# The conv branch of a hybrid encoder layer by Strassen's scheme, two gate groups at a time

## The chip, the cores and the metric

One core of one Trainium2 chip. The metric is the device time of one launch in microseconds, the median of several runs; smaller is better. The engines are TensorE (PE; its weight loads are shown as PEld), VectorE (DVE), ScalarE (ACT), GpSimd (POOL) and SyncE (SP), which here issues all DMAs of the stages that matter.

## The reference

One layer on x (1024 tokens x 1024), all in float32:

```python
u = rms_norm(x, norm1_g)
q, k, v, cb, cc, ch, ga, gb = split(u @ w_in)      # 3 x 512, 3 x 512, 2 x 1024
y_a = neighbourhood_attention(rms(q), rms(k), v, rpb) @ w_attn_branch     # 512 -> 1024
y_b = (cb * conv3(cc * ch)) @ w_conv_branch                              # 512 -> 1024
x = x + (sigmoid(ga) * y_a + sigmoid(gb) * y_b) @ w_o
x = x + square(relu(rms_norm(x, norm2_g) @ w_mlp_in)) @ w_mlp_out
```

The change concerns `y_b = b @ w_conv_branch` with `b = cb * conv3(cc * ch)`, and how its weights and those of the gates `ga`, `gb` are prepared beside the products.

## The kernel before

Every float32 product is made from f16 pairs: an operand is scaled by a power of two and split into a high and a low part (ScalarE copies the high part, VectorE subtracts it for the low one), and three passes of matmuls, high x high, low x high and high x low, are added up in PSUM. A unit is the group of matmuls that fills one PSUM bank; `unit` emits its matmuls (L236) and then moves the two background lists on by some steps: `fg`, work that is soon needed, and `bg`, the preparation of later weights, `ticks` steps a unit. So the order of all instructions is fixed when the program is built, and each engine works through its own list strictly in that order.

The preparation of a weight chunk, called a chain below: SyncE loads 512 KB into one of five `raw` tiles (L259) as soon as the tile's last reader is done; ScalarE scales it by rows (L1099) and sums its squares (L1108), or VectorE takes its largest absolute value (L362); a 128x1 matmul with a column of ones (L227, "ones matmul") sums over the partitions; VectorE makes a power of two of it; ScalarE and VectorE write the f16 high and low parts (L343 and L330, or L1238 and L1234). The ones matmul stands in TensorE's list between two units.

The stages: norm and transposes; V, Q, K projections; attention with the conv projections between its steps; gates and branches; O; two halves of the MLP. In the stage of the gates and branches the 1024 output channels are taken in eight groups of 128 (gate n = 0 to 7). Gate 0 (chunk G) is a plain product in units of 24 matmuls. Gates 1 to 7 (chunks S1 to S7) go by Strassen's scheme with seven units of 12 matmuls: the token halves and K halves of u stand ready in seven forms (`FORM`), made by DMA transposes from `gs` into `uT`, `QR` and `s4T`, and each gate's weights get seven forms: GpSimd makes the sums (`gsum`, L1221), `parts` splits them. After each gate come its branch units: attention (weights w_a, chunk A of two gate groups) and conv (weights w_b, chunk B), two token halves each, 12 matmuls a unit, plain. `post` multiplies by the gate, adds to `m`, and `m_done` scales and splits `m` for the O stage.

The conv rows of step j (0 to 3: 128 conv channels by 1024 tokens) are scaled, put in token order and split into the f16 pair `BT[:, w, j]` (bT in the profile) by `conv_split` during attention.

Of the kernel before, what the change touches and what calls it, by code (L numbers as in the profile page):

```python
# [18 lines left out]
D = 1024  # L19
# [9 lines left out]
def plan():  # L29
# [8 lines left out]
    branch = lambda j: [((k, j), block(w, [(256 * j, 256)], 4, 4)) for k, w in (("A", "w_a"), ("B", "w_b"))]  # L38
    for n in range(8):
        p.append((("S" if n else "G", n), block("w_in", [(3072 + 128 * n, 128), (4096 + 128 * n, 128)], 4)))  # L40
        if n % 2 == 0:
            p += branch(n // 2)
# [57 lines left out]
def encoder_block(ctx: ExitStack, tc: tile.TileContext, x, weights, cols, gqk, rel, masks, out):  # L100
# [745 lines left out]
    def conv_post(j, g, half, ps, d):  # L846
# [19 lines left out]
        cv = d["cv"]  # L866
        V.tensor_tensor(perm(cv, half), p3, perm(cv, half), op=OP.mult)
        if half == 1:
            conv_tail.append(conv_split(j, cv))
# [15 lines left out]
    def conv_split(j, cv):  # L885
        ch = cConv[j]
        m, s, inv = tmp(), tmp(), tmp()
        A.activation(BT[:, 1, j].bitcast(BF16), cv, AF.Square, accum_out=sc[:, m])
        yield
        V.tensor_scalar(sc[:, m], sc[:, m], 1e-36, None, op0=OP.max)  # L890
        yield
        yield from pow2_half(m, 14, s, inv)
        mul(inv, ch.inv, at(rowsB, j))
        if j == 3:
            for c in cB:
                c.ready = True
        G.tensor_scalar(cv, cv, sc[:, s], 1.0, op0=OP.mult, op1=OP.mult)
        yield
        bh, bl = (BT[:, w, j].rearrange("p (b r c) -> p b r c", b=8, r=16) for w in range(2))
        A.activation(bh, perm(cv), AF.Copy)  # L900
        yield
        pv = perm(cv)
        for b in range(0, 8, 2):
            G.tensor_tensor(bl[:, b:b + 2], pv[:, b:b + 2], bh[:, b:b + 2], op=OP.subtract)

    def conv_mms(first):

        for j in range(4):
# [3 lines left out]
            if 0 < j < 3:  # L912
                push(cConv[j + 1])
            elif j == 3:
                side[0], held[0] = True, 1
                push(cG, cA[0], cB[0])
# [155 lines left out]
    def turn_piece(i, o, m):  # L1072
        n, s = m // 2, m % 2
        SP.dma_start_transpose(free(o)(s)[:, :, 128 * n:128 * n + 128], GS[:, n, i, s])
# [61 lines left out]
    def deal(k):  # L1136
        room = 216.0 * share(k) + 520.0
        if conv_tail and not advance(conv_tail[0]):
            conv_tail.pop(0)
        for n in range(4):  # L1140
            if n and any(debt[i] + m.ns - mark[i] > room - 200.0 for i, m in enumerate(meters)):
                return
            tick(1)

    for k in range(N + 13):
# [28 lines left out]
        if 35 <= k < 59 and k % 3 == 2:  # L1174
            turn_piece(1, 0, (k - 35) // 3)
        if 69 <= k < 77:
            turn_piece(2, 2, k - 69)
# [13 lines left out]
    V, A = nc.vector, nc.scalar  # L1191
    solo[0] = False
# [4 lines left out]
    wpool["wa"] = wpool["wb"] = p3.enter_context(tc.tile_pool(name="wab", bufs=2))  # L1197
# [3 lines left out]
    actB = lambda s, k: BT[:, s, k]  # L1201
# [10 lines left out]
    turn_s(3, 6)  # L1212
# [15 lines left out]
    def parts(todo, s, then):  # L1228

        prev = None  # L1230
        for n, it in enumerate(todo + [None]):
            if prev:
                o, w = prev
                V.scalar_tensor_tensor(o(1), w, sc[:, s], o(0), op0=OP.mult, op1=OP.subtract)  # L1234
                then(n - 1)
            if it:
                o, w = it
                A.activation(o(0), w, AF.Copy, scale=sc[:, s])  # L1238
# [12 lines left out]

    def prep_s(n):

        ch = cS[n]
        t = w3p.tile([128, 4, 512], F32, name="gsum", bufs=1)
        if n == 1:
            while ch.s is None:
                yield WAIT
            yield from forms_sum(ch, t, None)
            s = ch.s  # L1260
        else:
            yield from rows_scaled(ch, g1)
            yield from forms_sum(ch, t, 2)
            s, ch.inv = yield from scale_of(ch.sum, 9, 2)
        while done[0] < ch.first:
            yield WAIT
        ch.P = wsp.tile([128, 7, 2, 512], F16, name="w16_s", tag="ws")
        yield from forms_split(ch, t, s, ch.P)
        ch.split = True
# [15 lines left out]
    def m_split(n, m, s):  # L1285
        A.activation(M[0][:, n], m, AF.Copy, scale=sc[:, s])
        yield
        V.scalar_tensor_tensor(M[1][:, n], m, sc[:, s], M[0][:, n], op0=OP.mult, op1=OP.subtract)

    def m_done(n, m):  # L1290
        mx, s = tmp(), tmp()
        V.tensor_reduce(sc[:, mx], m, axis=AX, op=OP.max, apply_absolute_value=True)
        yield
        yield from pow2(mx, 14, s, at(rowsM, n))
        yield from m_split(n, m, s)

    def gate_units(n, tail=None):
# [20 lines left out]
        def post3(ps):  # L1318
# [9 lines left out]
            7: post7, 3: post3}, 2, 4 if n < 7 else 6, (1, 6, 2, 4, 5, 7, 3))  # L1328
        return sg

    def branch_units(n, post, mid=None):
        j, cc = n // 2, (n % 2) * 128
        for g, act, ch in ((0, actA, cA[j]), (1, actB, cB[j])):
            built(ch)
            for half in range(2):
                ps = anybank()
                unit(ch_mms(ps, act, half, ch, 4, 256, cc),
                     lambda ps=ps, g=g, half=half, ch=ch: post(g, half, ps, sc[:, ch.inv]), 2, 4)
                if mid and g == 0 and half == 0:
                    mid()  # L1340

    for n in range(8):
        built(cG if n == 0 else cS[n])
        if n < 7:
            bg.append(prep_s(n + 1))
        m = w3p.tile([128, 2, 512], F32, name="m", bufs=1)
        mf = m.rearrange("p a t -> p (a t)")
        if n < 7:
            sg = gate_units(n)
            if n:  # L1350
                sg = [sg[:, i] for i in range(4)]
            if n in (1, 3, 5):
                push(cA[n // 2 + 1], cB[n // 2 + 1])

            def post(g, half, ps, iv, sg=sg, m=m):
                t = sg[2 * half + g]
                V.scalar_tensor_tensor(t, ps, iv, t, op0=OP.mult, op1=OP.mult)  # L1357
                if g == 1:
                    V.tensor_tensor(m[:, half], sg[2 * half], t, op=OP.add)
            branch_units(n, post, (lambda: turn_s(0, 2)) if n == 0 else None)  # L1360
            if n == 0:
                late.append(lambda: held.__setitem__(0, 0))
            late.append(lambda n=n, mf=mf: fg.append(m_done(n, mf)))
        else:
            push(cO[0])
            tick(4)
            y = w3p.tile([128, 4, 512], F32, name="gsum", bufs=1)
            branch_units(n, lambda g, half, ps, iv: A.activation(y[:, 2 * half + g], ps, AF.Copy, scale=iv))
            settle()
            drain()  # L1370
            s7 = tmp()

            def bound():
                mm, m2, mx = tmp(4), tmp(2), tmp()
                V.tensor_reduce(sc[:, mm], y, axis=AX, op=OP.max, apply_absolute_value=True)
                yield
                V.tensor_tensor(sc[:, m2], sc[:, mm.start:mm.start + 4:2], sc[:, mm.start + 1:mm.start + 4:2],
                                op=OP.add)
# [647 lines left out]
```

## Time and profile before

| | |
|---|---|
| time, median of 3 runs | 1200.63 us (1200.57 to 1201.13) |
| profiled execution | 1201.78 us |
| its span, first to last instruction | 1200.0 us |
| granted TensorE clock | 1.00 |
| PE busy | 1190.2 us, 99%, 6272 instructions |
| DVE, ACT, POOL busy | 78%, 63%, 38% |
| gates 1 on start at (timeline) | 332.13 us |
| O stage starts at (timeline) | 532.48 us |

A row of a group gives the line of the kernel, the engine, the operation, output and inputs by their names, sizes and count, then busy time and mean duration, then the idle time before it with what ended it. A row of a timeline gives the start, the duration, the same names, and in brackets the engine's idle time before it. SPq is SyncE's own queue: the time that an issue holds it.

### The profile page before, as it was taken

What the parts mean: (1) busy time and instruction counts of PE and PEld (TensorE: products, weight loads), DVE (VectorE), ACT (ScalarE), POOL (GpSimd) and SP (SyncE); (2) the same over time, 40 slices, a digit from 0 to 9 for tenths busy, and PEclk for the clock granted to TensorE, in tenths of its full rate; (3) what the DMA queues carried; (4) which work ended last, traced back from release to release, by engine and by line L of the source; (5) the groups of instructions that cost most, each with busy time, mean ns of one, the idle gap of its engine ahead of it and who ended that gap; (6) DMA issues with size and microseconds to landing.
All of it is one profiled execution on the core that took longest, in us unless ns stands there. A gap on an engine that the chain in (4) does not pass through costs nothing.

```text
span 1200.0 us, 16982 instructions
## 1 busy us (share of the span) xinstructions
PE 1190.2 (99%) x6272; PEld 574.7 (48%) x6272; DVE 940.3 (78%) x1750; ACT 752.1 (63%) x1181; POOL 450.9 (38%) x296
## 2 busy tenths in 40 slices
PE   8999999999999999999999999999999999999998
PEld 7444444444444444444467444444444444444444
DVE  7987878899558786877888645645548999999998
ACT  7765668778654545337778778678675843746440
POOL 5610022322311203001014665565567561564562
DMA  7745547576641121234397445435466925435202
GB/s 259 201 153 126 107 96 145 124 163 117 135 121 58 54 70 36 71 116 165 60 170 195 174 142 192 160 130 193 153 242 220 356 73 193 158 120 214 105 36 105
DMA packets 162707, 171.25 MB, mean 143 GB/s; under 512 B 123328, under 2 KB 123840, under 8 KB 158528
## 3 DMA queue, kind: packets, MB, share of 16 engines
q1 hardware_dynamic: 162624, 170.17, 48.4%
q8 instruction: 49, 0.80, 0.3%
q14 instruction: 34, 0.28, 0.1%
HBM read 102.51 MB, written 37.75 MB: 117 GB/s over the span
## 4 chain that ended last, share of the span: by engine, by line
PE 84%; DVE 11%; ACT 2%; issue 1%; DMA 1%; SPq 0%; ACTq 0%
PE ps_d L236 27%; PE ps_s L236 24%; PE ps_o L236 20%; PE ps_d L1067 5%; PE ps_d L669 2%; PE ps_d L718 2%; PE ps_s L718 2%; DVE P L95 2%; PE ps_s L669 2%; DVE w_s L1234 1%; DVE sz L95 1%; DVE sc L95 1%; DVE w_ws L95 1%; DVE sg L1357 1%; DMA xt<-in_x 1%
## 5 line engine op out<-in xcount | busy, mean ns | idle before, releaser
L236 PEld LDWEIGHTS <-ops 128*128 128x128 f16 x1356 | 132.5, 98 | 157.3
L236 PEld LDWEIGHTS <-w 128*128 128x128 f16 x1368 | 132.8, 98 | 139.4
L1067 PE MATMUL ps_d<-uT,w_ws 128*128 128x512 f16 x576 | 128.0, 379 | 0.3 <-DVE cv L95 0.3
L236 PE MATMUL ps_s<-ops 128*128 128x512 f16 (+1 forms) x504 | 114.3, 376 | 0.0
L236 PE MATMUL ps_d<-ops 128*128 128x512 f16 x492 | 112.9, 379 | 0.0
L236 PE MATMUL ps_d<-u2T,w 128*128 128x512 f16 (+1 forms) x504 | 110.1, 371 | 0.0
L1847 ACT ACTIVATE ops<-hf,sc 128x2048 f16<-128x2048 f32 x26 | 52.0, 1998 | 84.8 <-PE ps_d L236 47.2
L1221 POOL TENSOR_TENSOR tsum<-raw 128x512 f32<-128x512 f32 x28 | 48.2, 1737 | 139.3 <-DVE v L1475 74.2
L1425 POOL TENSOR_TENSOR as<-as 128x512 f32<-128x512 f32 x60 | 82.9, 1382 | 41.6 <-ACT as L1707 38.1
L236 PEld LDWEIGHTS <-w_s 128*128 128x128 f16 x588 | 56.8, 98 | 69.0 <-DVE w_s L1234 1.2
L1067 PEld LDWEIGHTS <-w_ws 128*128 128x128 f16 x576 | 54.6, 98 | 65.6 <-issue 1.5
L236 PE MATMUL ps_o<-ops 128*128 128x512 f16 (+1 forms) x360 | 81.3, 375 | 0.0
L236 PE MATMUL ps_s<-u2x,w 128*128 128x512 f16 (+1 forms) x348 | 78.6, 375 | 0.0
L1849 DVE SCALAR_TENSOR_TENSOR ops<-hf,sc,ops 128x2048 f16<-128x2048 f32 x26 | 74.8, 2876 | 3.2 <-ACT ops L1847 2.2
L1099 ACT ACTIVATE raw<-raw,sc 128x256 f32<-128x256 f32 x164 | 67.5, 494 | 1.9 <-DMA raw<-in_weights 1.9
L1221 POOL TENSOR_TENSOR gsum<-raw 128x512 f32<-128x512 f32 x14 | 19.3, 1394 | 127.8 <-issue 53.6
L1238 ACT ACTIVATE w<-raw,sc 128x512 f16<-128x512 f32 (+1 forms) x28 | 24.6, 927 | 50.8 <-DVE sc L475 50.8
L1740 DVE TENSOR_TENSOR as<-ps_s,as 128x512 f32<-128x512 f32 x13 | 9.0, 692 | 57.9 <-ACT as L1759 57.9
L1321 ACT ACTIVATE sg<-sg,sc 128x2048 f32<-128x2048 f32 (+1 forms) x7 | 13.2, 1880 | 52.2 <-DVE sg L1319 52.2
L1863 POOL TENSOR_TENSOR raw<-raw 128x1024 f32<-128x1024 f32 x8 | 30.8, 3870 | 36.5 <-DVE ops L1857 36.5
L236 PE MATMUL ps_o<-u2T,w 128*128 128x512 f16 (+1 forms) x204 | 44.2, 366 | 0.0
L236 PEld LDWEIGHTS <-mH 128*128 128x128 f16 x304 | 29.6, 98 | 30.4
(393 smaller groups left out, 2664.2 us busy)
## 6 DMA issues: line engine op xcount, KB each, us to landing
raw<-in_weights SPq DMA_DIRECT2D x89, 512.0 KB, 5.2
hs<-as SPq DMA_DIRECT2D x16, 1792.0 KB, 8.7
hf<-hs SPq DMA_DIRECT2D x26, 1024.0 KB, 6.6
w2x<-in_weights SPq DMA_DIRECT2D x16, 512.0 KB, 7.6
raw<-in_weights SPq DMA_DIRECT2D x16, 384.0 KB, 3.7
xt<-in_x SPq DMA_DIRECT2D x8, 512.0 KB, 10.2
gs<-s SPq DMA_DIRECT2D x4, 1024.0 KB, 4.4
x<-in_x SPq DMA_DIRECT2D x8, 512.0 KB, 10.6
```

The lines of the kernel that those rows point to most:

```text
L95: return f(out, *a, **kw)
L236: T.matmul(ps, l, r, start=a, stop=b)
L669: T.matmul(ps, UT[:, sa, k, b * 128:(b + 1) * 128], w, start=(kind, k) == ("hh", 0), stop=(kind, k) == ("hl", 7))
L718: T.matmul(vbank["q", b], UT[:, sa, k, b * 128:(b + 1) * 128], cQ.parts[:, sw, 512 * k:512 * k + 512], start=(k, n) == (0, 0), stop=(k, n) ...
L1067: T.matmul(ps, l, r, start=a, stop=b)
L1099: A.activation(v, v, AF.Copy, scale=sc[:, at(g, 4 * i + k)])
L1221: G.tensor_tensor(t[:, o], a, b, op=OP.add)
L1238: A.activation(o(0), w, AF.Copy, scale=sc[:, s])
L1425: sub.tensor_tensor(z[o], z[a], z[b], op=op)
L1847: A.activation(P[:, 1, 0], hf, AF.Copy, scale=sc[:, Rs])
L1849: V.scalar_tensor_tensor(P[:, 1, 1], hf, sc[:, Rs], P[:, 1, 0], op0=OP.mult, op1=OP.subtract)
L1863: G.tensor_tensor(w11[i2], w11[i2], w12[i2], op=OP.add)
```

## The change

The conv branch is made by Strassen's scheme over K (two halves: steps j of even and odd number), tokens (two halves) and output channels (two gate groups). For each of the four pairs of gate groups there are seven units of 6 matmuls in place of four units of 12.

- `conv_split` and `conv_forms` make seven forms of the conv rows for each half a = j // 2: per half two scalings, four sums and seven low parts on GpSimd, seven high copies on ScalarE, staged in four slots, and seven puts of 256 KB to a DRAM tile `BF` (bf in the lists).
- `land` reads a form back (512 KB) into one of four slots of the old bT space, four units ahead; it is issued once the unit that last read the slot is emitted.
- `prep_b` makes seven forms of a pair's w_b: ScalarE's squares, a ones matmul, four sums on GpSimd, eight splits.
- `ab(j)` emits a pair's B units and the four A units in a written order; `zb` holds the conv branch's four quarters; the addition of the two gated branches moves from VectorE to GpSimd (`join`); `m_done` takes ScalarE's sum of squares in place of VectorE's largest value, and `m` stays where the gates' products are.
- All chains S1, B0, S2, A1, S3, B1 and on go into one list `bg` at the stage's start. The loads of B chunks stand behind those of the odd S chunks.
- Gate 0 takes its second token half first, and its eight `uT` transposes follow that half; the transposes to `QR` and `s4T` are made with 8 x 128 columns in place of 4 x 128 (half as many). Gate 1 has its own order of units, 1, 6, 2, 4, 7, 5, 3. A0's units stay between gate 0 and gate 1; pair 0's B units come after gate 1.

```diff
+    def conv_forms(a, r):
+        for e in range(2):
+            G.tensor_scalar(CF[:, e], CF[:, e], sc[:, at(r, e)], 1.0, op0=OP.mult, op1=OP.mult)
...
+        hi(0, o1), hi(1, e0), hi(2, o0)
+        yield
+        lo(0, o1), lo(1, e0), lo(2, o0)
+        yield
+        G.tensor_tensor(o1, e1, o1, op=OP.subtract)
+        hi(3, o1)
+        yield
+        G.tensor_tensor(e1, e0, e1, op=OP.subtract)
+        G.tensor_tensor(e0, o1, e0, op=OP.subtract)
+        yield
+        put(0, 3), put(1, 0), put(2, 1)
+        lo(3, o1)
...
-    turn_s(3, 6)
+    for n in range(4):
+        SP.dma_start_transpose(s4T.rearrange("p s k t -> p (s k) t")[:, :, 128 * n:128 * n + 128],
+                               GS[:, n, 3].rearrange("p s c -> p (s c)"))
...
+    def prep_b(j):
+        ch = cB[j]
+        while not ch.raw or not formed[1]:
+            yield WAIT
...
+        for a in range(2):
+            A.activation(M[1][:, 6, :512].bitcast(BF16), raw[:, 512 * a:512 * a + 512], AF.Square,
+                         scale=sc[:, at(rowsB, a)], accum_out=sc[:, at(sm, a)])
+        yield
+        am = sum_of(sm)
...
-            for half in range(2):
+            for half in (1, 0):
                 ps = anybank()
                 unit(ch_mms(ps, actU, half, cG, 8, 256, 128), ...
+                if half:
+                    turn_s(0, 2)
...
+    def land(g):
+        if g < 28:
+            SP.dma_start(SLOT[:, g % 4], BF[:, SEVEN[ORDB[g % 7]][0]])
...
+        def b_unit(o):
+            i = ORDB[o]
+            w = {5: 6, 6: 5}.get(SEVEN[i][1], SEVEN[i][1])
+            act = SLOT[:, (7 * j + o) % 4]
+            ps[i] = anybank()
+            unit(group(ps[i], [(P[:, w, sw, 128 * a:128 * a + 128], act[:, a, sa]) for a in range(2)
+                               for sw, sa in PASSES]), posts.get(i), 2, 4)
+            land(7 * j + o + 4)
+        order = "bb0b1bbb2b3"
+        if j == 0:
+            order = "bbb2bb3bb"
...
+    bg.append(prep_s(1))
+    bg.append(prep_b(0))
+    for j in range(1, 4):
+        bg.append(prep_s(2 * j))
+        push(cA[j])
+        if j < 3:
+            bg.append(prep_s(2 * j + 1))
+        bg.append(prep_b(j))
```

The lists of the two programs give 12546 rows on TensorE before and 12498 now: 24 matmuls and 24 weight loads fewer. Three places show what moves.

SyncE from the last attention transposes to gate 1. Before, where raw_3679 and raw_3744 are the two parts of S2, raw_3773 is A1 and raw_3775 B1:

```order
L1023 DMA_TRANSPOSE PT_3463<-P16_3460 128x8x128
L1074 DMA_TRANSPOSE qD_965<-gs_112 128x4x128 x8
L1210 DMA_TRANSPOSE s4T_3634<-gs_112 128x4x128 x8
L259 DMA raw_3679<-in_weights 128x1024
L259 DMA raw_3744<-in_weights 128x1024
L1210 DMA_TRANSPOSE uT_109<-gs_112 128x4x128 x8
L259 DMA raw_3773<-in_weights 128x1024
L259 DMA raw_3775<-in_weights 128x1024
```

Now, where raw_3667 and raw_3723 are the parts of S2, raw_3725 is A1, bf the forms' puts and bT<-bf the first reads:

```order
L1119 DMA_TRANSPOSE qD_965<-gs_112 128x8x128 x2
L1260 DMA_TRANSPOSE s4T_3622<-gs_112 128x8x128 x4
L261 DMA raw_3667<-in_weights 128x1024
L922 DMA bf_1659<-bT_1197 128x1024 x3
L1257 DMA_TRANSPOSE uT_109<-gs_112 128x4x128 x8
L922 DMA bf_1659<-bT_1197 128x1024
L261 DMA raw_3723<-in_weights 128x1024
L261 DMA raw_3725<-in_weights 128x1024
L922 DMA bf_1659<-bT_1197 128x1024 x3
L1441 DMA bT_1197<-bf_1659 128x2048 x4
```

The second load of S2 and that of A1 stand behind the eight uT transposes, and puts stand between; the first load waits for the last of w_a's low parts.

VectorE at the start of gate 1. Before, between the end of m's chain and the first sums of gate 1 (sg_3811), one cast for a ones matmul, that of S2:

```order
L1326 TENSOR_TENSOR sg_3811<-ps_s_3840,sg_3811 128x512
L1288 SCALAR_TENSOR_TENSOR mL_3633<-m_3643,sc_71,mH_3632 128x1024
L1327 TENSOR_TENSOR sg_3811<-ps_o_3861,sg_3811 128x512
L1079 TENSOR_REDUCE sc_71<-sc_71 128x1
L1080 CAST ones_72<-sc_71 128x1
L1310 TENSOR_TENSOR sg_3811<-ps_o_3906,sg_3811 128x512
```

Now, from S1's last splits (w16_s_3678) on; the first cast is B0's, the next A1's, the last S2's:

```order
L1284 SCALAR_TENSOR_TENSOR w16_s_3678<-gsum_3673,sc_71,w16_s_3678 128x2x512 x2
L364 TENSOR_REDUCE sc_71<-raw_3725 128x4
L1468 SCALAR_TENSOR_TENSOR raw_3483<-ps_s_3734,sc_71,raw_3483 128x512
L1124 TENSOR_REDUCE sc_71<-sc_71 128x1
L1125 CAST ones_72<-sc_71 128x1
L152 TENSOR_TENSOR sc_71<-sc_71 128x4
L372 TENSOR_REDUCE sc_71<-sc_71 128x1
L374 CAST ones_72<-sc_71 128x1
L1468 SCALAR_TENSOR_TENSOR raw_3483<-ps_o_3762,sc_71,raw_3483 128x512
L1124 TENSOR_REDUCE sc_71<-sc_71 128x1
L1125 CAST ones_72<-sc_71 128x1
```

Three casts stand together behind the reduction of A1's load, ahead of gate 1's first sum; on TensorE B0's ones matmul stands right behind gate 1's first unit, where before no ones matmul came until six units of gate 1 were through.

ScalarE around the end of gate 1. Before, with gate 1's sigmoid first, S2's splits (w16_s_3959), the scaling of S3 (raw_3964, raw_3966) and its squares:

```order
L1321 ACTIVATE sg_3811<-sg_3811,sc_71 128x2048
L1238 ACTIVATE w16_s_3959<-raw_3679,sc_71 128x512
L1238 ACTIVATE w16_s_3959<-raw_3744,sc_71 128x2x512
L1238 ACTIVATE w16_s_3959<-gsum_3828,sc_71 128x2x512 x2
L1099 ACTIVATE raw_3964<-raw_3964,sc_71 128x2x128 x4
L1099 ACTIVATE raw_3966<-raw_3966,sc_71 128x2x128 x4
L1108 ACTIVATE gsum_4043,sc_71<-raw_3964 128x1024
L1108 ACTIVATE gsum_4043,sc_71<-raw_3966 128x1024
```

Now, with S2's splits (w16_s_3937) ahead of the sigmoid, S3 in raw_3890 and raw_3942, A1's high parts (w16_wa_3991) and B1's squares (raw_3944):

```order
L1288 ACTIVATE w16_s_3937<-gsum_3932,sc_71 128x2x512 x2
L1426 ACTIVATE sg_3786<-sg_3786,sc_71 128x2048
L1144 ACTIVATE raw_3890<-raw_3890,sc_71 128x2x128 x4
L1144 ACTIVATE raw_3942<-raw_3942,sc_71 128x2x128 x4
L1153 ACTIVATE mL_3621,sc_71<-raw_3890 128x1024
L1512 ACTIVATE zb_3627<-ps_d_3949 128x512
L345 ACTIVATE w16_wa_3991<-raw_3725,sc_71 128x256 x4
L1153 ACTIVATE mL_3621,sc_71<-raw_3942 128x1024
L1338 ACTIVATE mL_3621,sc_71<-raw_3944,sc_71 128x512 x2
```

S3's scaling now follows the sigmoid at once, with the chains of A1 and B1 in the same stretch; the cast that B1's ones matmul waits for needs the last row.

More of the change, by code (lines that the diff above doesn't have):

```diff
@@ L37, in plan @@
     p += [(("C", j), block("w_in", [(c + 128 * j, 128) for c in (2048, 2560, 1536)])) for j in range(4)]
[L38 removed]
+    branch = lambda k, w, j: (((k, j), block(w, [(256 * j, 256)], 4, 4)))
     for n in range(8):
@@ L1342, in encoder_block @@
[L1342 to L1363, printed above, removed]
+    ORDB = (1, 6, 2, 4, 5, 7, 3)
```

328 lines of the change are left out of this document (236 added, 92 removed).

## Prediction

> **What bounds the kernel now.** I read the page first: the busy times and the chain that ended last.
>
> ```profile
> span 1200.0 us, 16982 instructions
> ...
> PE 1190.2 (99%) x6272; PEld 574.7 (48%) x6272; DVE 940.3 (78%) x1750; ACT 752.1 (63%) x1181; POOL 450.9 (38%) x296
> ...
> PE 84%; DVE 11%; ACT 2%; issue 1%; DMA 1%; SPq 0%; ACTq 0%
> ```
>
> TensorE is busy for 99% of the span, so anything that takes a matmul away pays, and anything that makes TensorE wait costs in full. Then the table by stage, for the last 60 us of attention and the first gates (busy us, count, granted clock, DMA share).
>
> ```profile
> 240.00:270.00 30.00, 30.00 (x216) 14.61 (x213) 27.64 (x74) 22.33 (x53) 7.02 (x9) 1.00 0.77 163
> 270.00:300.00 30.00, 29.69 (x220) 14.89 (x220) 29.59 (x89) 24.84 (x62) 8.66 (x10) 1.00 0.65 117
> 330.00:360.00 30.00, 30.00 (x141) 13.58 (x140) 17.08 (x32) 15.00 (x26) 5.66 (x4) 1.00 0.43 121
> ```
>
> In the gates TensorE has no gap and VectorE is at 57%: there is room on average, and what decides is the moment at which each weight chain is ready. The timeline of TensorE at the place of the change, with its longest wait near the start of the program:
>
> ```profile
> 8.37 0.62 PE L598 MATMUL ps_o<-ident,u 128*128 128x128 f16 x8 [2.30 <-POOL u L585]
> ...
> 326.95 2.75 PE L236 MATMUL ps_d<-bT,w_wb 128*128 128x512 f16 x12
> 329.54 2.75 PE L236 MATMUL ps_s<-bT,w_wb 128*128 128x512 f16 x12
> 332.13 2.75 PE L236 MATMUL ps_d<-uT,w_s 128*128 128x512 f16 x12
> ```
>
> A unit of 12 matmuls starts 2.59 us after the one before, 0.216 us a matmul. Gate 1 starts at 332.13.
>
> **What is removed.** The conv branch has 8 x 2 x 12 = 192 matmuls before and 4 x 7 x 6 = 168 after. 24 x 0.216 = 5.2 us off TensorE. Two of the old B units stood ahead of gate 1 and now stand behind it, so gate 1 begins at 326.95 and its first unit ends at 329.54, on before's clock.
>
> **Gate 1, first stall.** Behind that unit stands the ones matmul of the first B chunk. It waits for VectorE's cast, and VectorE reaches the cast only past the reduction over the first part of A1's weights (raw_3725), whose load SyncE issues behind eight uT transposes; the squares that feed the cast stand on ScalarE behind the scaling of gate 2's second part (raw_3723), whose load stands behind them too. Before, both loads of gate 2 stood ahead of those transposes:
>
> ```profile
> 314.44 11.07 SPq L1210 DMA_TRANSPOSE s4T<-gs x8
> 325.62 0.99 SPq L259 DMA_DIRECT2D raw<-in_weights x2
> 326.70 10.36 SPq L1210 DMA_TRANSPOSE uT<-gs x8
> 337.17 1.46 SPq L259 DMA_DIRECT2D raw<-in_weights x3
> ```
>
> A transpose holds SyncE for 1.3 us, a load for 0.5. The rows for the rest of the chain, from the timelines of ScalarE, GpSimd and VectorE:
>
> ```profile
> 312.59 1.71 ACT L343 ACTIVATE w_wa<-raw,sc 128x256 f16<-128x256 f32 x4 [0.31 <-POOL bT L904]
> 329.86 3.30 ACT L1099 ACTIVATE raw<-raw,sc 128x256 f32<-128x256 f32 x8 [1.88 <-DMA raw<-in_weights]
> 307.72 1.12 POOL L897 TENSOR_SCALAR cv<-cv,sc 128x1024 f32<-128x1024 f32 x1 [10.71 <-DVE sc L95]
> 309.57 0.35 DVE L95 TENSOR_TENSOR sc<-sc 128x1 f32<-128x1 f32 x2
> 313.13 5.30 DVE L330 SCALAR_TENSOR_TENSOR w_wa<-raw,sc,w_wa 128x256 f16<-128x256 f32 x4 [2.71 <-ACT w_wa L343]
> 323.09 1.68 DVE L330 SCALAR_TENSOR_TENSOR w_wb<-raw,sc,w_wb 128x256 f16<-128x256 f32 x4 [3.89 <-ACT w_wb L343]
> ```
>
> and the groups of the gates' stretch, with the mean of one:
>
> ```profile
> L1321 ACT ACTIVATE sg<-sg,sc 128x2048 f32<-128x2048 f32 x6 | 12.0, 2003 | 50.8 <-DVE sg L1319 50.8
> L1108 ACT ACTIVATE gsum<-raw 128x1024 f32<-128x1024 f32 x12 | 12.6, 1053 | 0.2
> L1108 ACT ACTIVATION_READ_ACCUMULATOR gsum<-raw 128x1 f32 x12 | 2.2, 187 | 0.0
> L1325 ACT ACTIVATE sg<-ps_d 128x512 f32<-128x512 f32 x3 | 1.8, 590 | 0.8 <-PE ps_d L236 0.8
> L1221 POOL TENSOR_TENSOR gsum<-gsum,raw 128x512 f32<-128x512 f32 x14 | 18.0, 1285 | 3.0 <-ACT gsum L1108 2.4
> L1234 DVE SCALAR_TENSOR_TENSOR w_s<-gsum,sc,w_s 128x1024 f16<-128x1024 f32 x14 | 17.3, 1277 | 0.0
> L1234 DVE SCALAR_TENSOR_TENSOR w_s<-raw,sc,w_s 128x1024 f16<-128x1024 f32 x7 | 9.0, 1283 | 1.7 <-ACT w_s L1238 1.7
> L1234 DVE SCALAR_TENSOR_TENSOR w_s<-raw,sc,w_s 128x512 f16<-128x512 f32 x7 | 5.3, 751 | 10.0 <-ACT w_s L1238 9.9
> L1310 DVE TENSOR_TENSOR sg<-ps_s,sg 128x512 f32<-128x512 f32 x3 | 2.1, 688 | 10.4 <-PE ps_d L227 5.2 <-PE ps_o L227 5.2
> L1357 DVE SCALAR_TENSOR_TENSOR sg<-ps_d,sc,sg 128x512 f32<-128x512 f32 x8 | 5.9, 742 | 0.0
> L1288 DVE SCALAR_TENSOR_TENSOR mL<-m,sc,mH 128x1024 f16<-128x1024 f32 x7 | 9.9, 1417 | 2.9 <-ACT mH L1286 2.9
> L362 DVE TENSOR_REDUCE sc<-raw 128x4 f32<-128x1024 f32 x6 | 7.3, 1211 | 0.0
> L158 DVE TENSOR_SCALAR sc<-sc 128x1 int32<-128x1 int32 x16 | 2.4, 152 | 0.4
> ```
>
> The chain, in before's time. VectorE has the conv factors at 309.9. GpSimd scales two halves (2 x 1.12 = 312.2); ScalarE's first high part 0.6; three low parts and the first difference 4 x 1.285 = 317.9; its high part 0.6 = 318.5. Only then, in ScalarE's order, come w_a's four high copies, 1.71 = 320.2. VectorE's four low parts follow: they took 1.68 us with GpSimd idle and 5.30 with GpSimd at its sums. So they end between 320.6 and 324.2 (TensorE wants the last of them at 323.9: at most 0.3 us lost), and they release gate 2's first load. On SyncE: that load and three puts of forms 4 x 0.49 = 1.95, eight transposes 10.36, a put and the second load 0.97: issued between 334.0 and 337.5. Landing, as from 325.62 to 329.86, 4.24: 338.2 to 341.7. ScalarE: four scalings 1.65, two squares 2 x 1.24, two half squares 2 x 0.78; VectorE's reduction and cast 0.3: 344.2 to 347.7. TensorE stands there since 329.54: 14.7 to 18.2 us. GpSimd is at the forms all through w_a's low parts, so the row of 5.30 is the nearer one: I take 17. Behind the ones matmul TensorE's queue holds the other six units of gate 1 and all that follows, so nothing fills the gap. What else is late there hides under it: the low parts of gate 1's gsum, the rest of the forms with their puts, and the first reads of the forms.
>
> **Pair 0, second stall.** Counted from the end of the first. Gate 1's unit 5 is over at 5 x 2.59 = 13.0; VectorE does three sums (0.69 each, 15.2), three of gate 2's splits (0.75 + 1.28 + 1.28, 18.5) and the last sum (19.2). Then ScalarE in order: sigmoid 2.0, eight scalings of gate 3's weights 3.30, a square 1.24, a copy 0.59, w_a's high copies 1.71, a square 1.24, the two half squares of the next B chunk 1.56; cast 0.3: 31.1. TensorE is at the ones matmul that needs them after 114 matmuls, 24.6. Stall 6.5; 3.8 if the three splits did not stand ahead of the sigmoid, 8 if they meet GpSimd as w_a did.
>
> **Gates 2 and 3, third stall.** From pair 0's last sums of the conv branch to the cast for the third B chunk's ones matmul, which stands among pair 1's units, VectorE has the splits of three gates (3 x (0.75 + 1.28 + 2 x 1.277) = 13.8), 15 sums from PSUM (10.3), three gatings (2.2), two low parts of m (2.8), 12 pieces of w_a and w_b (4.8), a reduction (1.2) and 45 small ones (6.8): 41.9 us, and 2.8 of sums ahead of it. TensorE has 198 matmuls there, 42.7. So 2.0 us if VectorE never idled; 5.6 at the 92% that it reached in 240 to 270; 14 at the page's 78%. Each step waits for ScalarE or a load, so zero is out; I take 5.6.
>
> **The rest.** Fewer, larger transposes and the joins on GpSimd stand in queues that nothing waits for: zero, up to 4 us together if GpSimd's 9 us of the first conv half (two scalings, seven to eight ops) block VectorE where it is at 27.64 of 30. Gates 4 to 7 have their chains done ahead by the one list: zero, 3 if the same pattern comes back.
>
> **A rule beside it.** The longest wait of TensorE in this trace is 2.30 us, with a granted clock of 1.00 throughout, so no row shows what a longer one does. The Trainium skill (TensorE: Matmul & The Clock Gate, Part 1: The HAM clock gate) says that an idle window of about 3.4 us halves TensorE's clock until it has been busy for as long again. By that page the sum would be about 1.7 us higher for each of the three stalls, 1231 in all (an estimate from its figures).
>
> **The sum.** 1201.78 - 5.2 + 17 + 6.5 + 5.6 = 1225.7 for a profiled execution. Its span is 1200.0 and 1.78 lie around it; the median of the runs, 1200.63, is 1.15 lower, so 1224.5. With all lower ends 1216, with all upper ones 1236.
>
> **Rivals.** A measurement of this kernel tells about 0.2%, 2.4 us, from no change.
> - *The 24 matmuls are all that counts* (faster, 0.12). The first ones matmul is the place: the wait is hidden if the transposes' 10.36 us is not spent on SyncE, w_a's low parts are free of GpSimd (-3.6) and the loads land within the 2 us that they are issued early. It decides once the three stalls together are under 5.2 us; with none of them 1195.4. For it: all of before's ones matmuls cost nothing. Against: the SPq rows show SyncE held 1.3 us for each transpose at a time when all that they need was long done.
> - *The gain and a short first stall cancel* (within 0.2%, 0.03): 5 us in sum, about 1200.
> - *Only the first stall* (0.15): the 17 us pause lets the other engines run ahead, and the later two go. 1201.78 - 5.2 + 8 to 17 - 1.15 = 1203 to 1212. Against: the second is counted from the first one's end.
> - *TensorE comes back slow* (0.20): after each stall one unit at half the rate, 5.18 us in place of 2.59, three times: 1224.5 + 7.8 = 1232. The page above states such a rule; the trace neither bears it out nor speaks against it.
> - *More stalls behind* (0.08): the first conv half slows attention and gates 4 to 7 stall as pair 1 does, 7 to 20 us: 1232 to 1245.
> - That the change does not do what it says is out: the counts of matmuls are in the program.
>
> **Numbers.** My forecast has 0.42. The range leaves out the faster and equal cases (0.15) and the upper end of the last: 1204 to 1243. Faster 0.12, same 0.03, slower 0.85.
>
> **What would show it.** TensorE idle for 14 to 18 us before the ones matmul behind gate 1's first unit, released by VectorE's cast; in SyncE's row eight uT transposes of 10 us ahead of two loads; ScalarE waiting for a load just then; w_a's low parts at over 4 us; two shorter gaps within the next 100 us; 24 matmuls fewer. I am wrong if TensorE runs through gate 1, if the wait there ends on something else (the forms' reads, w_a), or if the clock falls.

## Result and profile after

| | before | after |
|---|---|---|
| time, median of 4 runs each | 1200.88 us (1200.57 to 1201.22) | 1256.69 us (1255.21 to 1257.34) |
| ratio, 95% interval | | 1.0463 (1.0445 to 1.0481) |
| span of the profiled execution | 1200.0 us | 1255.3 us |

The change costs 55.8 us. The forecast of 1224.5 had the sign and the first wait, and lies 32 us too low; the time is also above the range's end of 1243. Line numbers below are those of the changed kernel: a matmul of `unit` is L238 there, the ones matmul L229.

The page of the changed kernel: busy times, TensorE and its clock in 40 slices of 31 us, the chain.

```profile
span 1255.3 us, 17139 instructions
...
PE 1198.5 (95%) x6248; PEld 577.1 (46%) x6248; DVE 956.7 (76%) x1775; ACT 777.6 (62%) x1241; POOL 504.0 (40%) x332
...
PE   8999999989767759999999999999999999999998
...
PEclk9999999999978879999999999999999999999999
...
PE 81%; DVE 7%; ACT 5%; POOL 3%; issue 2%; DMA 1%; SPq 1%; POOLq 0%; DVEq 0%; ACTq 0%
```

TensorE has its 24 matmuls less, but its idle time rose from 9.8 to 56.8 us, and its busy time rose by 8.3, though 24 matmuls fewer would lower it by 5.2: some of its matmuls ran slower. Both lie in slices 9 to 15, attention's end and gates 0 to 3. Its timeline there, with the wait in brackets:

```profile
334.52 2.75 PE L238 MATMUL ps_d<-uT,w_s 128*128 128x512 f16 x12
...
355.07 0.16 PE L229 MATMUL ps_s<-ones 128*128 128x1 bf16 x1 [17.80 <-DVE ones L1125]
355.10 4.39 PE L238 MATMUL ps_d<-qD,w_s 128*128 128x512 f16 x12
...
381.88 1.47 PE L238 MATMUL ps_o<-bT,w_wb 128*128 128x512 f16 x6 [1.62 <-DMA bT<-bf]
...
388.37 0.16 PE L229 MATMUL ps_d<-ones 128*128 128x1 bf16 x1 [5.03 <-DVE ones L1125]
388.40 4.80 PE L238 MATMUL ps_s<-qD,w_wa 128*128 128x512 f16 x12
...
425.86 0.16 PE L229 MATMUL ps_s<-ones 128*128 128x1 bf16 x1 [6.61 <-DVE ones L374]
425.89 4.83 PE L238 MATMUL ps_o<-uT,w_s 128*128 128x512 f16 x12
...
459.08 0.16 PE L229 MATMUL ps_s<-ones 128*128 128x1 bf16 x1 [12.78 <-DVE ones L1125]
459.10 2.72 PE L238 MATMUL ps_d<-bT,w_wb 128*128 128x512 f16 x6
461.62 4.06 PE L238 MATMUL ps_s<-qD,w_wa 128*128 128x512 f16 x12
```

Four waits end at a ones matmul, 42.2 us together, and one at the read of a form. Each of the four is followed by matmuls at a lower rate: a unit of 12 takes 4.06 to 4.83 in place of 2.75. The unit behind the 1.62 us for a form runs at full rate. Gate 1's first unit starts at 334.52, where before's clock would have had it at 326.95. The whole loss by term:

| term | forecast | measured |
|---|---|---|
| 24 matmuls fewer | -5.2 | -5.2 |
| attention ends later | 0, up to 4 | 7.6 |
| first wait, in gate 1 | 17 (14.7 to 18.2) | 17.80 |
| second, in pair 0 | 6.5 (3.8 to 8) | 5.03 + 1.62 |
| third, gates 2 and 3 to the third B chunk's sum | 5.6 (2 to 14) | 6.61 + 12.78 |
| slow units behind the waits | 0 (rival: 7.8) | 1.64 + 2.05 + 2.08 + 1.26 + 1.31 = 8.3 |
| gates 4 to 7 | 0 | 0 |
| sum | 23.9 | 54.5 of 55.3 |

The first wait has the chain that the prediction wrote down. SyncE, ScalarE and VectorE of the changed kernel:

```profile
332.60 11.22 SPq L1257 DMA_TRANSPOSE uT<-gs  x8
...
344.55 0.87 SPq L261 DMA_DIRECT2D raw<-in_weights  x2
349.17 1.70 ACT L1144 ACTIVATE raw<-raw,sc 128x256 f32<-128x256 f32 x4 [6.84 <-DMA raw<-in_weights]
326.00 4.66 DVE L332 SCALAR_TENSOR_TENSOR w_wa<-raw,sc,w_wa 128x256 f16<-128x256 f32 x4 [8.70 <-ACT w_wa L345]
351.00 1.22 DVE L364 TENSOR_REDUCE sc<-raw 128x4 f32<-128x1024 f32 x1 [8.70 <-DMA raw<-in_weights]
354.87 0.16 DVE L1125 CAST ones<-sc 128x1 bf16<-128x1 f32 x1
```

Eight transposes of 1.4 us stand ahead of the two loads, ScalarE and VectorE wait for these, and the low parts of w_a took 4.66 us beside GpSimd.

### The profile page after: what moved, and what is told of

Its sections match the earlier page's. It is cut to its first block, busy times and chain, and to the rows that moved or that the text cites. A ratio compares the mean times of both kernels' runs of the same rounds, so it can differ in the third digit from the quotient of the medians.

```text
span 1255.3 us, 17139 instructions
## 1 busy us (share of the span) xinstructions
PE 1198.5 (95%) x6248; PEld 577.1 (46%) x6248; DVE 956.7 (76%) x1775; ACT 777.6 (62%) x1241; POOL 504.0 (40%) x332
## 4 chain that ended last, share of the span: by engine, by line
PE 81%; DVE 7%; ACT 5%; POOL 3%; issue 2%; DMA 1%; SPq 1%; POOLq 0%; DVEq 0%; ACTq 0%
PE ps_d L238 25%; PE ps_s L238 22%; PE ps_o L238 18%; PE ps_d L1112 6%; PE ps_d L671 2%; PE ps_d L720 2%; PE ps_s L720 2%; PE ps_s L671 1%; DVE w_s L1284 1%; PE ps_o L1093 1%; SPq L1257 1%; ACT w_s L1288 1%; PE ps_s L1017 1%; ACT raw L1144 1%; POOL raw L1356 1%
## 5 line engine op out<-in xcount | busy, mean ns | idle before, releaser
L238 PEld LDWEIGHTS <-ops 128*128 128x128 f16 x1356 | 132.5, 98 | 157.3
L238 PEld LDWEIGHTS <-w 128*128 128x128 f16 x1368 | 132.9, 98 | 139.4
L238 PE MATMUL ps_s<-ops 128*128 128x512 f16 (+1 forms) x528 | 119.7, 377 | 0.0
L238 PE MATMUL ps_d<-ops 128*128 128x512 f16 x480 | 110.1, 379 | 0.0
L238 PEld LDWEIGHTS <-w_s 128*128 128x128 f16 x588 | 57.8, 99 | 96.4 <-ACT mL L1338 18.1
L238 PE MATMUL ps_d<-u2T,w 128*128 128x512 f16 (+1 forms) x360 | 78.8, 368 | 0.0
L238 PE MATMUL ps_o<-ops 128*128 128x512 f16 (+1 forms) x348 | 78.6, 375 | 0.0
L1144 ACT ACTIVATE raw<-raw,sc 128x256 f32<-128x256 f32 x164 | 67.8, 493 | 16.4 <-DMA raw<-in_weights 14.7
L238 PE MATMUL ps_o<-u2T,w 128*128 128x512 f16 (+1 forms) x348 | 76.0, 368 | 0.0
L238 PE MATMUL ps_s<-u2x,w 128*128 128x512 f16 (+1 forms) x336 | 74.5, 371 | 0.0
L1489 POOL TENSOR_TENSOR sg<-sg 128x512 f32<-128x512 f32 x12 | 16.4, 1378 | 83.1 <-DVE sg L1479 60.5
L2025 POOL TENSOR_TENSOR t<-raw,w2x 128x1024 f32<-128x1024 f32 x6 | 18.8, 3138 | 61.8 <-DMA w2x<-in_weights 61.8
L238 PEld LDWEIGHTS <-mH 128*128 128x128 f16 x304 | 29.6, 98 | 30.4
```

The source lines that it names most:

```text
L238: T.matmul(ps, l, r, start=a, stop=b)
L1144: A.activation(v, v, AF.Copy, scale=sc[:, at(g, 4 * i + k)])
L2025: G.tensor_tensor(T2[:, i], w12[i], w22[i], op=OP.add)
```

## Experiments

Each kernel is one edit on the changed kernel unless it says otherwise; before ran on the same chip at 1201.1 to 1201.3 each time. The interval of a ratio is 0.0015 to 0.0018 on either side.

### Is the lower rate the clock after a wait?

The granted clock in the changed kernel, in stretches of 5 us (the eighth column is the clock):

```profile
345.00:350.00 5.00, 0.00 (x0) 0.00 (x0) 0.00 (x0) 0.83 (x3) 0.00 (x0) 0.50 0.89 250
350.00:355.00 5.00, 0.00 (x0) 0.00 (x0) 2.17 (x5) 4.93 (x12) 0.00 (x0) 0.50 0.98 352
355.00:360.00 5.00, 4.92 (x17) 1.90 (x17) 2.42 (x14) 0.13 (x1) 0.00 (x0) 0.66 0.59 234
```

The first experiment fills three of the four waits with matmuls that nobody reads:

```diff
+    FILL = {1: 80, 3: 21, 7: 57}
+        for _ in range(FILL.get(turns[0], 0)):
+            T.matmul(bk, QD[:, 0, 0, 0:128], QD[:, 0, 0, 0:512], start=True, stop=True)
```

> The changed kernel with dummy matmuls (128x512, results overwritten) ahead of three of the four ones matmuls that TensorE waited for: 80 before the first (wait 17.8 us), 21 before the second (5.0), 57 before the fourth (12.8); none before the third (6.6), which is the control. If idle time is what halves TensorE's clock: granted clock 1.00 and 2.59 us for the unit behind each filled wait (4.2, 4.6 and 3.9 before), still about half rate behind the third; 1.6 + 2.0 + 2.5 us less in all, part of which the next chain may take back: 1250 to 1253 us. If the clock falls for another reason: the same slow units and 1256 to 1258 us.

Measured: 1251.07 us, ratio 1.0415. A unit behind the first filled wait, then the third wait, which was not filled, and the unit behind it, in TensorE's timeline:

```profile
353.48 0.16 PE L229 MATMUL ps_s<-ones 128*128 128x1 bf16 x1 [0.56 <-DVE ones L1128]
353.50 2.75 PE L238 MATMUL ps_d<-qD,w_s 128*128 128x512 f16 x12
...
420.59 0.16 PE L229 MATMUL ps_s<-ones 128*128 128x1 bf16 x1 [6.61 <-DVE ones L374]
420.62 4.77 PE L238 MATMUL ps_o<-uT,w_s 128*128 128x512 f16 x12
```

Units run at 2.75 us where TensorE had had something to do, and at 4.77 behind the wait that was left open. So an idle TensorE loses its clock. The units behind the three filled waits take 1.64, 2.05 and 2.57 us less in this profile, 2.1 us a wait, beside the 1.7 that the Trainium skill's rule (TensorE: Matmul & The Clock Gate, Part 1: The HAM clock gate) gave as an estimate. The trace agrees with it on the halved clock, 0.50. It does not agree that this takes an idle window of about 3.4 us: in attention the clock fell too (see the section on attention below), behind single waits of at most 1.82 us.

The 5.6 us between the medians are not a clean price of the clock. Gate 1 starts at 332.90 in this profile and at 334.52 in the changed kernel's, with nothing changed ahead of it, and the last filling ends 1.0 us after the cast that it stood for.

### What made the first wait?

Two edits, each alone: the transposes of `turn_s(0, 2)` issued behind A's units of gate 0, and B0's chain not held until the second half's forms stand.

```diff
-                if half:
-                    turn_s(0, 2)
...
     for half in range(2):
         a_unit(0, half)
+    turn_s(0, 2)
```

> The eight uT transposes issued after A0's units instead of behind gate 0's first half, so that gate 2's second load and A1's load stand ahead of them in SyncE's order. If SyncE's 11.2 us on them are in the chain of the first wait: that wait falls from 17.8 to 6 or 7 us, and a new one of 3 to 6 us comes at gate 1's unit 5, which reads what they write: 1248 to 1252 us. If the chain hangs on the conv forms and w_a instead, the wait stays at 15 us or more and the time at 1255 to 1258.

```diff
-        while not ch.raw or not formed[1]:
+        while not ch.raw:
```

> The preparation of the first B chunk no longer waits for the conv forms, so its ones matmul is emitted ahead of gate 1 and the next ones matmul stands behind gate 1's fourth unit. If the place of the ones matmul is what counts: the first wait falls from 17.8 to 7 or 8 us (that of A1's reduction, whose load is as late as before), and the time to 1245 to 1249. If the wait only moves into the later ones because the chains of gate 2, A1 and B1 are as late as before: 1254 to 1257.

Measured: 1248.53 and 1249.54 us; the first wait fell to 10.94 and to 8.21. So SyncE's queue and the late start of B0's chain each hold a part of it. The parts do not add up to the whole: with both edits at once (the run with all three shifts, below) the wait is still 8.01 us. There VectorE casts B0's sum behind S1's last splits, for which it had waited 4.15 us for ScalarE, and ScalarE stood behind the high copies of the forms. The prediction had named the forms and S1's low parts as work that hides under this wait. In the second kernel part of what it won came back at once, 2.75 us at the next sum and 3.80 at the read of a form.

### Where do the attention's 7.6 us go?

VectorE's groups in 230 to 290 us, of before and then of the changed kernel (out<-in, count | busy, mean ns of one):

```profile
L95 DVE SCALAR_TENSOR_TENSOR P<-sz,sc,P 128x384 f16<-128x384 f32 x20 | 13.2, 658 | 0.0
L95 DVE SCALAR_TENSOR_TENSOR w_ws<-raw,sc,w_ws 128x384 f16<-128x384 f32 x8 | 5.9, 755 | 0.2 <-ACT w_ws L95 0.2
```

```profile
L97 DVE SCALAR_TENSOR_TENSOR P<-sz,sc,P 128x384 f16<-128x384 f32 x16 | 12.8, 802 | 0.0
L97 DVE SCALAR_TENSOR_TENSOR w_ws<-raw,sc,w_ws 128x384 f16<-128x384 f32 x8 | 7.8, 990 | 0.2 <-ACT w_ws L97 0.2
```

The same operations take 22% and 31% longer while GpSimd makes forms. TensorE waits 5.3 us there for VectorE, at most 1.82 us at a time, and the granted clock falls once, to 0.66 over these 5 us:

```profile
275.00:280.00 5.00, 4.49 (x35) 2.79 (x35) 4.89 (x21) 4.38 (x13) 0.00 (x0) 0.66 0.48 91
```

So besides the waits the 7.6 us hold up to 1.7 us of lower clock (an estimate, 0.34 of 5 us). The size varies: in eight profiles of kernels that are alike up to here gate 1 starts between 332.90 and 334.74, 6.0 to 7.8 us late. The edit leaves out the seven low parts of each half:

```diff
-            G.tensor_tensor(STG[:, n, 1], v, STG[:, n, 0], op=OP.subtract)
+            pass
```

> The conv forms without their low parts on GpSimd (7 subtractions per half left out, the low parts are zero). If GpSimd's work is what slows the end of attention, by blocking VectorE: gate 1's first unit starts 3 to 5 us earlier than 334.5 and the waits on VectorE in attention (4.8 us in three) fall under 2; w_a's low parts take under 3 us in place of 4.7; 1248 to 1252 us. If the puts, the scalings or SyncE's order slow attention: gate 1 starts at 333 or later and the time is 1254 to 1257.

Measured: 1248.68 us, ratio 1.0394. Gate 1's first unit in the timeline, and the group:

```profile
328.06 2.75 PE L238 MATMUL ps_d<-uT,w_s 128*128 128x512 f16 x12
```

```profile
L97 DVE SCALAR_TENSOR_TENSOR P<-sz,sc,P 128x384 f16<-128x384 f32 x20 | 13.7, 687 | 0.0
```

The attention loses 1.1 us in place of 7.6, and the mean of the group goes back from 802 to 687 ns. So GpSimd's low parts hold up these operations of VectorE, which read two SBUF inputs; before, VectorE had 2.4 us to spare in 30 there. The Trainium skill (SBUF — State Buffer, Who interferes with whom) puts VectorE and GpSimd on a shared pair of ports; these rows agree.

### Why 19.4 us in gates 2 and 3?

The last wait is for B2's sum, a pair ahead of the units that use it. Its squares were done 15 us before its cast, which stood in VectorE's list behind the splits of A2 and S5 and five gate sums (timelines of ScalarE and VectorE, changed kernel):

```profile
443.80 0.19 ACT L1338 ACTIVATION_READ_ACCUMULATOR mL<-raw,sc 128x1 f32 x1
...
442.39 4.70 DVE L332 SCALAR_TENSOR_TENSOR w_wa<-raw,sc,w_wa 128x256 f16<-128x256 f32 x4
...
458.87 0.16 DVE L1125 CAST ones<-sc 128x1 bf16<-128x1 f32 x1
```

A2's low parts took 4.70 us there, beside GpSimd's sums for S5, in place of 1.68 before: 3.0 us of the 12.78 at most are this. No run takes this part away alone.

So the first theory was the place of the sums. The edit moves those of A and B chunks to 8 and 10 units behind the measure; then all three shifts (the two edits on the first wait and this one, with the S chunks' sums moved as well) at once, with less and with more distance. The one with more distance is called the far version.

```diff
-        s, ch.inv = yield from scale_of(am, 0, 1)
+        s, ch.inv = yield from scale_of(am, 0, 10 if j else 1)
...
-                yield from apart(units[0], 3 if self.kind != "O" else ...)
+                yield from apart(units[0], 8 if self.kind == "A" else 3 if ...)
```

> Of the changed kernel only the distance between a cast and its ones matmul is larger from pair 1 on: at least 10 units for B1 to B3 (1 before) and 8 for A1 to A3 (3 before); nothing is left out. TensorE then comes to the ones matmuls of A2 and B2 some 25 us of matmuls later. If their early place is the cause of the third wait: the 6.6 and 12.8 us go, or fall under 5 together, the first two stay near 18 and 5, and the time is 1232 to 1238 us. If VectorE has too much work for the matmuls of that stretch, wherever the ones matmuls stand: the wait moves to gate 3's or 4's weights and the time is 1248 or more.

> B0's preparation early, the uT transposes after A0's units, and ones matmuls later (8 units for B1 to B3 and for A, 3 for S in place of 2). If the three waits are separate and each has the cause that I give it: first wait under 4 us, second under 3, third under 5; clock losses under 2; the attention stage keeps its 6 to 8: 1208 to 1220 us. If the waits pass on what is taken away: 1230 or more.

> As the run before it, with longer distances: 10 units for B1 to B3, 6 for S and 8 for A. If distance alone is what lacks: equal to the run before or up to 5 us faster, 1205 to 1220 us. If a chain then comes too late for its own gate: a wait on w_s or w_wb in place of one on the cast, and 5 to 15 us slower than the run before.

Measured: 1255.08, 1254.12 and 1241.08 us. The gains that were hoped for (1232 to 1238, 1208 to 1220, 1205 to 1220) came in none of them, though the far version is 13 us faster than the one with less distance: most of the waits left the sums and came back at weights, forms and PSUM banks. The most direct trial leaves the sums out, on the changed kernel and on the far version:

```diff
+        if not solo[0]:
...
+            V.tensor_scalar(sc[:, out], a, floor, None, op0=OP.max)
+            yield
+            return
         T.matmul(bk[:, 0:1], ones[:, 0:128], a, start=True, stop=True)
```

> The changed kernel with the ones matmuls of all weight chains from gate 0 on left out: each partition is scaled by its own sum, so TensorE no longer stands in line for a sum; the places and the order of everything else stay. The four waits at such matmuls are 17.8, 5.0, 6.6 and 12.8 us, 42.2 in all. Theory 1 (TensorE is stopped too early, at the measure of weights that it needs only a unit's or a gate's time later, and the list is otherwise in time): the 42.2 us shrink to under 15, at weights or forms, and the lower clock behind the waits goes with them: 1205 to 1222 us. Theory 2 (the list of weight chains is itself late, sums or not, because its steps wait for one another across ScalarE, VectorE and GpSimd): TensorE stops a unit or two later at the weights themselves, idle stays above 30 us, and the time stays above 1238.

> The version of the run with all three shifts and the far sums (1241), with the ones matmuls of all weight chains from gate 0 on left out as in the run with own sums. Theory 1 (the sums' places): with the first chain early as well little is left to wait for: 1200 to 1212. Theory 2 (the list is late): what waits in the far version at a sum (8.0, 2.7, 5.1 us) moves on to the weights and forms: 1234 to 1242.

Measured: 1247.29 and 1237.42 us. Both are what theory 2 gave. The place of the sums explains 9 us of the changed kernel's loss, not the 35 to 52 that theory 1 gave. What TensorE waits for without any sum (us in total, times, longest):

```profile
PE ps_d L244 <- DVE sg L1423: 9.5, 1, 9.5
PE ps_d L244 <- DMA bT<-bf: 6.6, 1, 6.6
...
PE ps_o L244 <- DMA bT<-bf: 4.7, 1, 4.7
PE ps_d L244 <- ACT w_s L1294: 2.7, 1, 2.7
```

9.5 us go to a PSUM bank whose reader, a gate sum, stands in VectorE's list behind the splits of S4 and A2. In the far version without sums the longest wait is 13.61 us, for ScalarE's high parts of a gate's weights. And the pace of the list is the same. From the second square of m to the low parts of A2's w_a, the changed kernel and the one without sums, busy us of TensorE, its weight loads, VectorE, ScalarE, GpSimd:

```profile
402.77:442.47 39.70, 33.09 (x146) 14.39 (x145) 26.96 (x62) 27.97 (x48) 13.80 (x12) 0.91 0.24 69
```

```profile
396.59:436.30 39.71, 34.96 (x162) 15.63 (x160) 26.97 (x62) 27.98 (x48) 13.81 (x12) 1.00 0.22 69
```

The list needs 39.7 us for this stretch whether TensorE stands at sums or not, and neither VectorE (68%) nor ScalarE (70%) is full. What they wait for, in 340 to 460 us of the changed kernel, VectorE and then ScalarE:

```profile
DVE w_s L1284 <- ACT w_s L1288: 9.2, 7, 4.2
DVE sc L364 <- DMA raw<-in_weights: 8.7, 1, 8.7
DVE w_wb L1284 <- ACT w_wb L1288: 5.1, 5, 1.2
```

```profile
ACT sg L1426 <- DVE sg L1424: 9.8, 2, 7.3
ACT mL L1387 <- POOL raw L1489: 8.5, 1, 8.5
ACT w_s L1288 <- DVE sc L477: 8.3, 3, 3.8
ACT w_wb L1288 <- POOL raw L1356: 7.7, 4, 3.5
ACT raw L1144 <- DMA raw<-in_weights: 6.8, 1, 6.8
```

VectorE waits mostly for ScalarE, and ScalarE for VectorE and, nearly as long, for GpSimd. Two trials then asked what a step more or less on an engine does: GpSimd's four sums of each B chain left out; those sums and the joins moved to VectorE, on the changed kernel and on the far version.

```diff
-            G.tensor_tensor(w[:, o[0], o[1]], ...)
+            pass
```

> The changed kernel without GpSimd's four sums for the forms of w_b (left out, so four of the seven forms are wrong). In the third stretch VectorE, GpSimd, ScalarE and VectorE hand this chunk on one after the other for 6 us ahead of A2's reduction. If it is this hand-over and not VectorE's load that makes the wait: the 6.6 us fall to 2 or 3 and the second wait of that stretch stays within 1.5 us of 12.8: 1250 to 1253 us. If VectorE's load does: no change, 1255 to 1258.

```diff
-            G.tensor_tensor(w[:, o[0], o[1]], ...)
+            V.tensor_tensor(w[:, o[0], o[1]], ...)
...
-            G.tensor_tensor(t, t, part(n, 2 * half + 1), op=OP.add)
+            V.tensor_tensor(t, t, part(n, 2 * half + 1), op=OP.add)
```

> The changed kernel with the joins of the A and B products and the four sums of each B chain moved from GpSimd to VectorE: VectorE gets about 0.7 us for each of 14 joins and 0.4 us for each of 16 sums more, and ScalarE's waits behind GpSimd in the stretch from 340 to 460 us of the changed kernel (8.5 and 7.7 us and 1.7 at rows that GpSimd releases) become waits behind VectorE. Theory A (the list is late because its steps hand over from engine to engine, and a step on a slower engine holds the next): 1248 to 1254 us. Theory B (VectorE has too much work there, as the prediction had it): 1257 to 1263.

> The version with all three shifts and the far sums (1241) with the same joins and sums on VectorE. Theory A (hand-overs): 1232 to 1238. Theory B (VectorE's work): 1242 to 1247.

Measured: 1254.94, 1256.00 and 1235.85 us. On the changed kernel neither moves the time by more than its interval: leaving out the sums changes nothing, as expected if this hand-over is not what makes the wait, and moving them fell between the two theories' ranges. On the far version the move won 5.2 us, as theory A had it. With VectorE's steps added to the changed kernel the stretch reads

```profile
394.50:459.00 64.50, 46.16 (x205) 20.22 (x203) 50.75 (x102) 39.56 (x67) 11.73 (x9) 0.88 0.30 93
```

against this row of the changed kernel:

```profile
394.50:459.04 64.54, 45.20 (x202) 19.80 (x201) 46.42 (x94) 38.41 (x64) 24.02 (x19) 0.88 0.28 85
```

The rows are cut at the same times. Cut at the same two instructions (the first sum of the conv branch at the left, B2's cast at the right) the stretch is 63.7 us with 50.0 of VectorE's work against 64.5 with 46.4: 3.6 us more work and no longer. VectorE's amount of work is not the bound; and with GpSimd out of those steps ScalarE waits as long for others, among them the weight loads, 9.8 us for 6.8 before the edit:

```profile
ACT raw L1144 <- DMA raw<-in_weights: 9.8, 2, 6.7
```

Last, how many steps of the list stand behind each unit: four in place of five, as before the change, and seven (five behind a B unit).

```diff
-..., 2, 5 if n < 7 else 6, ...)
+..., 2, 4 if n < 7 else 6, ...)
```

> The changed kernel with four steps of the list behind each unit of gates 1 to 6 and of A, as before the change, for five: the list's operations stand later in each engine's order, the sums of the operations on gate sums earlier against them; in the order the sums of A2, B2 and so on stand 2 to 8 us of matmuls later. Theory C (the list stands too early in the engines' orders: VectorE and ScalarE do weights that are not yet needed ahead of the gate sums that hold PSUM banks, and TensorE stands at sums of weights far off): 1235 to 1250. Theory D (the list is late for TensorE's need, so it should stand earlier, not later): 1258 to 1275.

> The version with all three shifts and the far sums (1241) with four steps behind each unit for five. Theory C: 1228 to 1238. Theory D: 1243 to 1260.

> The changed kernel with seven steps of the list behind each unit of gates 1 to 6 and of A and five behind a B unit, for five and four. Theory D (the list is late, and how many of its steps are put behind a unit sets how late): gain about as four steps lost (7.6 us), less what the sums, which now stand 2 to 8 us of matmuls earlier, stop: 1246 to 1255. Theory E (the list is held by its own hand-overs and the waits just move to the sums): 1256 to 1266.

> The version with all three shifts, the far sums and GpSimd's steps on VectorE (1235.9) with seven and five steps. Theory D: what waits there for weights (5.8 us) and a PSUM bank behind ScalarE (5.0 us) shrinks: 1222 to 1230. Theory E: 1234 to 1242.

Measured: 1264.24 and 1256.33 us with four, 1279.51 and 1246.29 with seven, the latter on the version with VectorE's steps (1235.85). Both directions lose. Four steps came out as theory D had it, seven in neither theory's range. With four steps the far version waits for weights (5.90 and 8.05 us), the changed kernel at other sums (9.90 and 9.55). With seven the changed kernel reaches sums that are not ready:

```profile
434.47 0.16 PE L229 MATMUL ps_s<-ones 128*128 128x1 bf16 x1 [15.03 <-DVE ones L374]
```

The number of steps moves the waits about; no change of it won anything.

### Do the parts add up?

The low parts of the forms left out of the far version, and of the version with seven steps:

> The version with all three shifts and the far sums (1241) with the seven low-part subtractions of each half of the forms left out (the low parts are zero), as in the run without low parts. If what GpSimd takes from VectorE in the attention and what the list takes behind it are separate, the 6 to 7 us of the attention go and the rest stays: 1233 to 1236. If gate 1's start only moves ahead of a list that is late for it, the wait behind it grows by as much: 1239 to 1242.

> The version of the run before with the low-part subtractions of the forms left out as well. If the attention's part is separate as it was in the far version: 6 to 8 us less than that run; if it still stays above 1201, what is left are the first wait and the weights.

Measured: 1234.09 us against 1241.08, and 1239.13 against 1246.29: 7.0 and 7.2 us, close to the 6.5 by which gate 1 came earlier in the run without low parts alone. That part is separate from the rest. Among the versions that leave no work out the best is the far one with VectorE's steps, 1235.85 us, ratio 1.0290 (1.0275 to 1.0305): 20.8 us better than the change, 34.5 worse than before. Nothing tried beats before.

## Why the prediction was right or wrong

- **24 matmuls, first wait:** right, in place, releaser, chain and size. The two edits show that SyncE's queue and the late start of B0's chain are both in it; 8.0 us of it stay without either.
- **Second wait:** right in place and releaser. The close sum, 6.65 for 6.5, is in part luck: 5.03 us are this wait, and 1.62 ended on the read of a form, which the prediction had put under the first wait.
- **Third wait:** wrong, 19.4 for 5.6, beyond its upper end of 14 and in two places, at A2's sum as well as at the B2 sum that was forecast. This is the largest step that failed, 13.8 us. The prediction took the stall as VectorE's work divided by the share of the time that it reaches, 92% as in attention. The work was near, 41.9 + 2.8 us forecast and 46.42 measured (3.0 of these for A2's slowed low parts); the share measured is 72%, and with it the prediction's sum, 41.9 / 0.72 + 2.8 - 42.7, gives 18.3. But that share is the length of the stretch turned round, not its cause: with 3.6 us more of VectorE's work the stretch was no longer, and VectorE's share rose to 78%. What the runs show in place of this step is that the list takes its time whether TensorE stands at sums or not (39.70 and 39.71 us); why it takes that long is not settled.
- **The rest of attention:** wrong, 7.6 for 0, at most 4. The prediction had the mechanism, GpSimd blocking VectorE, and had used its price on w_a; it put none of it into the sum where VectorE was at 27.64 of 30 us. The run without low parts shows 6.5 of the 7.6 to be this term.
- **The clock:** it stood as a rival, with 7.8 us; it measured 8.3 behind the waits in the gates. That these are close is luck: the rival had 2.6 us for each of three waits, and four waits came with 1.6 to 2.6 each. Since the forecast itself had three waits longer than any in the trace, this was a term of the sum, and it was put at nothing. Filling three of the waits showed it.
- **The rivals:** that the gain stays alone, that it cancels, and that only the first wait comes are all out. Of the last rival the slower attention came, the waits in gates 4 to 7 did not.

What stays open: which step of the list one would have to shorten. The runs show that it is not the sums' place alone, not VectorE's amount of work, not GpSimd's B sums, and not the number of steps behind a unit; that the hand-overs between ScalarE and VectorE set the pace is what the equal 39.7 us and the two tables of waits suggest, but it is not shown: leaving out GpSimd's B sums did not make the kernel faster, and moving them to VectorE shortened the stretch by 0.8 us only. Nor was a list tried that serves the gates in before's order with the seven B forms.

## What to carry over

Where work for later is woven into the lists of several engines in a fixed order, do not cost it as one engine's work over a share borrowed from another stage: 92% for 72% was 13 us here, and the share itself changed with the work while the stretch did not. Follow the hand-overs from engine to engine instead, as the prediction did for the first wait, which it got right. A wait put into TensorE's list costs its length and then about 2 us of clock, and moving it is no cure as long as the chain behind it keeps its pace: the wait turns up at the next thing that is needed. Against a preparation that had just kept up, 24 matmuls, 5.2 us, are little.

## Not expected of the hardware

A transpose of SyncE cost about 1.4 us in these rows whatever its size: four for `s4T`, each twice as large as before, held SyncE for 5.82 us, where the eight before had taken 11.07; the eight for `uT`, of the old size, still took 11.22. TensorE's granted clock falls to 0.50 in the waits of the gates, down to the one of 5.03 us, and stays there for a unit behind them; in attention it fell behind waits of 1.82 and 0.22 us; a 128x384 operation of VectorE went up to 1.70 us beside GpSimd.

```profile
315.94 5.82 SPq L1260 DMA_TRANSPOSE s4T<-gs  x4
...
240.10 1.70 DVE L97 SCALAR_TENSOR_TENSOR P<-sz,sc,P 128x384 f16<-128x384 f32 x1
```
